# Cached keys, cached values and broadcast queries loaded through GpSimd's queue

## The chip, the core and the metric

The kernel runs on one core of a Trainium2 chip. The metric is device time in microseconds from start to end of the program. The kernel before takes 1567.99 us, the median of 3 runs (1566.31 to 1571.45).

A core has five engines that each take instructions from a queue of their own, in order: TensorE (PE, with weight loads shown as PEld), VectorE (DVE), ScalarE (ACT), GpSimd (POOL) and SyncE (SP). A DMA is issued by an instruction that stands in the queue of one of these engines; the bytes are then moved by 16 DMA engines that all issuers share. In the kernel before, nearly all transfers are issued from SP, some stores from ACT, and none from POOL.

## The reference

One step of a two-layer decoder trunk for a prompt of 512 tokens and for 8 sample sequences of 8 tokens with 2048 tokens of history. Layer 0 mixes tokens by dilated attention, layer 1 by a diagonal state-space layer; each is followed by a gated feed-forward block. The change lies in the attention of the sample sequences, which reads cached keys and values:

```python
DIL_GROUPS = ((128, 1), (512, 4), (2048, 16))     # (window, dilation)
def dilated_block(q_blk, kv_all, qi, dilation, n_keys):
    idx = qi[:, None] - dilation * jnp.arange(n_keys)[None, :]
    kvg = jnp.take(kv_all, jnp.maximum(idx, 0), axis=1)
    ...
    s = jnp.einsum('bqhd,bqkhd->bqhk', q_blk, kf) * (HEAD_DIM ** -0.5)
    lse = jax.nn.logsumexp(s, axis=-1)
    o = jnp.einsum('bqhk,bqkhd->bqhd', jnp.exp(s - lse[..., None]), vf)
# per token: softmax over the three groups' lse, weighted sum of the three o, then @ w_o
```

For each of 8 sequences and each of the three groups the scores need the cached keys at the group's stride, and the outputs need the cached values at the same places. New caches, shifted by 8 tokens, are outputs too.

## The kernel before

**Stages.** The program runs through these stages, one after the other on TensorE:

- 0 to about 300 us: the projection to queries, keys and values. Nine chunks of 512 columns; each weight piece (`raw`, L87) is split into a high and a low part (ACT L99, DVE L100) and multiplied in three passes (L353 to L355). Between the pieces the scores of the sample sequences are computed: group 2 on VectorE (`products`, L394: a tile of cached keys `kc` times a tile of queries `qb` copied to all 128 partitions, L399, then a sum per head, L401), groups 1 and 0 on TensorE (`score`, transposes L486, products L490 and L493).
- about 300 to 329 us: the rest of the scores of group 0 (eight sequences, one tile of 256 KB each).
- 329 to about 461 us, called the attention stage here: `attn_phase`. Four pairs of heads of the prompt (`prompt_pair`: scores L631, L634, L638, softmax on ACT and DVE, transposes L647, outputs L654 and L660) and eight decodes (`decode`, one for each sequence: seven tiles of cached values, 3328 KB in all, multiplied in L700, closed by L703 and a transpose L707). The last three sequences' scores of group 2 are computed here as well, now with the multiplication on GpSimd (L399) and the sum on VectorE.
- 461 us to the end: output projection, feed-forward, state-space layer, feed-forward. These stages load no cached keys or values.

**Buffers.** Cached keys, cached values and broadcast queries share a pool `kst` of six buffers of 512 KB, all named `kc`; the group-2 products of the attention stage have four buffers of their own in pool `kpa`, also named `kc`. Weights have four `raw` buffers.

**What sets the order.** The code says what depends on what; a scheduler, which plays the program through with its own estimate of each instruction's duration, then writes one fixed order per engine. Every engine works its order off without overtaking: an instruction that waits for a semaphore holds up all that stand behind it on the same engine. SP's order mixes the weight pieces (L87), the cached tiles (L390), the broadcast queries (L398), the prompt's values `vt` (three loads of 1 MB each, L588), a mask `mp` (512 KB, L586), the samples' new values `vn` (L690) and copies of the caches to the outputs (L83).

Of the kernel before, what the change touches and what calls it, by code (L numbers as in the profile page):

```python
# [29 lines left out]
WIN = (128, 512, 2048)  # L30
# [10 lines left out]
def dram(ap, off, dims):  # L41
    return bass.AP(tensor=ap.tensor, offset=ap.offset + off, ap=[list(d) for d in dims])
# [339 lines left out]
CACHES = ("cache_kv_w128", "cache_kv_w512", "cache_kv_w2048")  # L382
# [4 lines left out]
def cache_tile(nc, A, pool_, name, gi, b, c0, n, kv):  # L387
    t = pool_.tile([128, 2, 512], F32, name=name)[:, :n]
    st = STRIDE[gi]
    nc.sync.dma_start(t, dram(A[CACHES[gi]], (b * WIN[gi] + c0) * 1024 + kv * 512, [[st * 1024, 128], [1024, n], [1, 512]]))  # L390
    return t


def products(nc, A, L, eng, kst, P, b, part):  # L394
    c0 = 2 * part
    kc = cache_tile(nc, A, kst, "kc", 2, b, c0, 2, 0)
    qb = kst.tile([128, 2, 512], F32, name="kc")
    nc.sync.dma_start(qb, dram(L["qscr"], (b * 8 + c0) * 512, [[0, 128], [512, 2], [1, 512]]))  # L398
    eng.tensor_tensor(kc, kc, qb, OP.mult)  # L399
    for c in range(2):  # L400
        nc.vector.tensor_reduce(P[:, :, 0:2, c0 + c], kc[:, c].rearrange("p (a h d) -> p a h d", a=4, h=2), AX.X, OP.add)  # L401
# [17 lines left out]
def qkv_phase(nc, tc, A, es, L):  # L419
# [36 lines left out]
    def score2(b, part):  # L456
        if part == 0:
            prods[b] = dk.tile([128, 4, 4, 8], F32, name="P2", bufs=1)
            g.memset(prods[b], 0.0)
        products(nc, A, L, v, kst, prods[b], b, part)  # L460
        if part == 3:
            close2(nc, L, dk, psd, "Sd", prods.pop(b), b)

    def score(gi, b):
# [14 lines left out]
        for c0 in range(0, n, 2):  # L479
            w = min(2, n - c0)  # L480
            kc = cache_tile(nc, A, kst, "kc", gi, b, c0, w, 0)
            for c in range(w):
                u = c0 + c
                kp = ptp.tile([128, 4, 128], F32, name="pt")
                for hp in range(4):
                    te.transpose(kp[:, hp, :], kc[:, c, hp * 128:(hp + 1) * 128], ident)  # L486
                ks = dk.tile([128, 4, 128], F32, name="ks")
                s.activation(ks, kp, AF.Copy)
                for hp in range(4):
                    te.matmul(Sd[hp * 32:hp * 32 + 32, 0:128], Q[:, u, hp, :], ks[:, hp, :], start=u == 0, stop=u == n - 1,  # L490
                              tile_position=(0, hp * 32), skip_group_check=True)
# [100 lines left out]
def attn_phase(nc, tc, A, es, L):  # L592
# [71 lines left out]
    def decode(b):  # L664
# [28 lines left out]
        for gi in (0, 1, 2):  # L693
            for c0 in range(0, UNITS[gi], 2):
                w = min(2, UNITS[gi] - c0)
                vc = cache_tile(nc, A, kst, "kc", gi, b, c0, w, 1)
                for c in range(w):
                    for hp in range(4):
                        pz = pa[:, hp, :] if u == 0 else Z[:, u - 1, hp, :]
                        te.matmul(O[hp * 32:hp * 32 + 32, :], pz, vc[:, c, hp * 128:hp * 128 + 128], start=u == 0, stop=False, tile_position=(0, hp * 32), skip_group_check=True)  # L700
                    u += 1
# [14 lines left out]
    def score2():  # L716
        if not rest:
            return
        b, part = rest.pop(0)
        if part == 0:  # L720
            prods[b] = dk.tile([128, 4, 4, 8], F32, name="P2", bufs=1)
            g.memset(prods[b], 0.0)
        products(nc, A, L, g, kp, prods[b], b, part)
        if part == 3:
            close2(nc, L, dk, pD, "Sd", prods.pop(b), b)
# [628 lines left out]
```

## Time and profile before

| | |
|---|---|
| median of 3 runs | 1567.99 us |
| profiled execution, time / span | 1569.92 us / 1568.1 us |
| TensorE busy | 1517.8 us (97%) |
| VectorE busy | 917.3 us (58%) |
| ScalarE busy | 522.0 us (33%) |
| GpSimd busy | 320.6 us (20%) |
| DMA packets of SP's queue | 57.0% of the 16 engines' span, 305.86 MB |
| cached tiles issued (L390) | 96 of 512 KB, 16 of 256 KB |
| broadcast queries issued (L398) | 32 of 512 KB |

The span runs from the first to the last instruction. Busy time of TensorE includes modelled ends, so a busy TensorE is not one at its peak. DMA issues are not counted as busy time of the engine that issues them; a row such as `SPq` shows them.

### The profile page before, as it was taken

The page shows a single profiled execution, that of the slowest core. Times are in us where ns is not written, and L with a number is a line of the kernel's source. Part 1 is how long each engine was busy: PE and PEld are TensorE (multiplying, and loading weights), DVE is VectorE, ACT ScalarE, POOL GpSimd, SP SyncE. Part 2 cuts the span into 40 slices and gives each one's busy share as a digit, 9 for nine tenths or more (in the row PEclk, how much of TensorE's full clock was granted, in tenths as well). Part 3 has the DMA queues.
Part 4 walks back from the last instruction along what each step waited for, and adds up shares of the span by engine and source line. Part 5 has one row for each costly group of instructions (what it writes and reads, how often), then busy time and mean ns, then how long its engine had stood idle before and what let it go on. Part 6 is the DMA issues. An engine that isn't in the chain of part 4 may idle for free.

```text
span 1568.1 us, 28963 instructions
## 1 busy us (share of the span) xinstructions
PE 1517.8 (97%) x12038; PEld 1405.5 (90%) x12038; DVE 917.3 (58%) x1661; ACT 522.0 (33%) x774; POOL 320.6 (20%) x343
## 2 busy tenths in 40 slices
PE   9989899889979999999999999999999999999998
PEld 7878688656659999999999999999999999999998
DVE  5788954558727865388869666764343333333332
ACT  4524344634415221222212254343242212221222
POOL 2000102323203013845335420021011001000100
PEclk9999999988979999999999999899999999999999
DMA  7396853797985656488676665865545556442212
GB/s 264 129 368 229 268 186 108 230 349 248 322 265 162 221 195 222 165 314 285 243 242 235 240 223 183 269 181 202 218 164 208 192 187 217 154 144 81 81 62 81
DMA packets 194323, 326.79 MB, mean 208 GB/s; under 512 B 39568, under 2 KB 137104, under 8 KB 192656
## 3 DMA queue, kind: packets, MB, share of 16 engines
q1 hardware_dynamic: 184112, 305.86, 57.0%
q10 hardware_dynamic: 10080, 19.08, 3.5%
q8 instruction: 94, 1.54, 0.4%
q14 instruction: 37, 0.30, 0.1%
HBM read 291.31 MB, written 120.88 MB: 263 GB/s over the span
## 4 chain that ended last, share of the span: by engine, by line
PE 53%; DVE 2%; DMA 1%; ACT 0%; issue 0%; ACTq 0%; DVEq 0%
PE acc L106 49%; PE aux L106 1%; DMA u_scr<-uP 1%; DVE cb L1048 1%; DVE kk L1057 1%; PE acc L1138 1%; PE acc L1176 0%; PE acc L1177 0%; PE aux L1041 0%; PE aux L1177 0%; PE aux L1052 0%; PE aux L1176 0%; PE aux L814 0%; DVE Z L1158 0%; PE aux L1058 0%
## 5 line engine op out<-in xcount | busy, mean ns | idle before, releaser
L100 DVE TENSOR_TENSOR wlo<-raw,whi 128x1024 fp32r<-128x1024 f32 x200 | 247.1, 1236 | 274.3 <-ACT whi L99 266.6
L99 ACT ACTIVATE whi<-raw 128x1024 fp32r<-128x1024 f32 x200 | 208.1, 1042 | 515.6 <-PE acc L106 401.6
L106 PE MATMUL acc<-xgl,whi 128*128 128x288 f32 x1760 | 378.9, 296 | 0.0
L106 PE MATMUL acc<-xgh,whi 128*128 128x288 f32 x1760 | 377.2, 296 | 0.1
L106 PE MATMUL acc<-xgh,wlo 128*128 128x288 f32 x1760 | 377.2, 295 | 0.0
L106 PEld LDWEIGHTS acc<-xgl,whi 128*128 128x128 f32 x1760 | 282.7, 188 | 1.2 <-issue 1.0
L106 PEld LDWEIGHTS acc<-xgh,wlo 128*128 128x128 f32 x1760 | 282.9, 188 | 0.6 <-issue 0.2
L106 PEld LDWEIGHTS acc<-xgh,whi 128*128 128x128 f32 x1760 | 281.5, 188 | 0.5 <-DVE gt L791 0.3
L793 POOL TENSOR_TENSOR gt<-gt,rstd 128x576 f32<-128x576 f32 x44 | 79.9, 1817 | 429.0 <-ACT gt L792 428.9
L106 PE MATMUL acc<-hh,whi 128*128 128x288 f32 x704 | 151.3, 296 | 0.0
L106 PE MATMUL acc<-hh,wlo 128*128 128x288 f32 x704 | 151.2, 295 | 0.0
L106 PE MATMUL acc<-hl,whi 128*128 128x288 f32 x704 | 150.8, 295 | 0.0
L354 PE MATMUL acc<-wlo,xh 128*128 128x512 f32 x288 | 115.5, 403 | 3.4 <-DVE wlo L100 3.4
L353 PE MATMUL acc<-whi,xh 128*128 128x512 f32 x288 | 108.4, 400 | 5.6 <-ACT a L569 4.2
L106 PEld LDWEIGHTS acc<-hh,wlo 128*128 128x128 f32 x704 | 113.1, 188 | 0.2 <-issue 0.2
L106 PEld LDWEIGHTS acc<-hl,whi 128*128 128x128 f32 x704 | 113.0, 188 | 0.2 <-issue 0.2
L106 PEld LDWEIGHTS acc<-hh,whi 128*128 128x128 f32 x704 | 113.1, 188 | 0.0
L355 PE MATMUL acc<-whi,xl 128*128 128x512 f32 x288 | 112.9, 399 | 0.0
L191 POOL TENSOR_TENSOR ssum<-ssum,sq 128x576 f32<-128x576 f32 x21 | 36.1, 1717 | 180.8 <-ACT sq L190 180.8
L353 PEld LDWEIGHTS acc<-whi,xh 128*128 128x128 f32 x288 | 54.6, 191 | 19.1 <-ACT a L569 5.1
L354 PEld LDWEIGHTS acc<-wlo,xh 128*128 128x128 f32 x288 | 55.3, 192 | 15.7 <-DVE wlo L100 4.4
L355 PEld LDWEIGHTS acc<-whi,xl 128*128 128x128 f32 x288 | 55.3, 192 | 11.2
(351 smaller groups left out, 2017.4 us busy)
## 6 DMA issues: line engine op xcount, KB each, us to landing
o_kv_s<-cache_kv_w SPq DMA_DIRECT2D x64, 1020.0 KB
kc<-cache_kv_w SPq DMA_DIRECT2D x96, 512.0 KB
raw<-ffn_w_gate SPq DMA_DIRECT2D x44, 512.0 KB
raw<-ffn_w_up SPq DMA_DIRECT2D x44, 512.0 KB
raw<-ffn_w_down SPq DMA_DIRECT2D x40, 512.0 KB
raw<-w_qkv SPq DMA_DIRECT2D x36, 512.0 KB
kc<-qscr SPq DMA_DIRECT2D x32, 512.0 KB
o_kv_s<-cache_kv_w SPq DMA_DIRECT2D x16, 1008.0 KB
```

Source lines behind the costliest of these rows:

```text
L99: s.activation(hi, raw, AF.Copy)
L100: mark[0] = v.tensor_tensor(lo, raw, hi.bitcast(F32), OP.subtract)
L106: te.matmul(ps[:, c, :HN], w, x[:, c * HN:(c + 1) * HN], start=first and i == 0, stop=last and i == 2)
L191: g.tensor_tensor(self.ss, self.ss, sq, OP.add)
L353: te.matmul(ps[t], ah, wh[:, k2, :], start=k == 0, stop=False)
L354: te.matmul(ps[t], ah, wl[:, k2, :], start=False, stop=False)
L355: te.matmul(ps[t], al, wh[:, k2, :], start=False, stop=k == KT - 1)
L793: g.tensor_tensor(t, t, nin.r, OP.mult)
L1048: v.tensor_copy(cb[i][hs, :, gl, :], c[hs, qs, :])
L1057: v.scalar_tensor_tensor(k7, dmask, dcol[:, f:f + 1], k7, op0=OP.mult, op1=OP.add)
L1138: te.matmul(S[gl * 64:gl * 64 + 64, ri, q * 72:q * 72 + 72], Wc[:, ri, q, gl * 64:gl * 64 + 64], U[:, 2 * q + gl, :], start=True, stop=True)
```

## The change

The two lines that issue the loads of cached tiles and of broadcast queries name GpSimd instead of SyncE. All 112 loads of L390 and all 32 of L398 move: 144 DMAs. Weights, `vt`, `mp`, `vn` and the copies to the outputs stay on SP.

```diff
 def cache_tile(nc, A, pool_, name, gi, b, c0, n, kv):
     t = pool_.tile([128, 2, 512], F32, name=name)[:, :n]
     st = STRIDE[gi]
-    nc.sync.dma_start(t, dram(A[CACHES[gi]], ...))
+    nc.gpsimd.dma_start(t, dram(A[CACHES[gi]], ...))
     return t
...
     qb = kst.tile([128, 2, 512], F32, name="kc")
-    nc.sync.dma_start(qb, dram(L["qscr"], ...))
+    nc.gpsimd.dma_start(qb, dram(L["qscr"], ...))
     eng.tensor_tensor(kc, kc, qb, OP.mult)
```

Since the scheduler runs again, the order of the engines changes with it, up to the end of the attention stage; behind it all orders are as before. Three places matter.

SP at the entry to the attention stage, before. `kc` are cached tiles, `vt` the prompt's values, `mp` a mask, `o_kv_s` an output copy:

```order
L83 DMA o_kv_s<-cache_kv_w 16x16320
L390 DMA kc<-cache_kv_w 128x512 x2
L586 DMA mp<-c_mp 128x2048
L588 DMA vt_3181<-vtscr 128x4x512
L390 DMA kc<-cache_kv_w 128x512
L588 DMA vt_3180<-vtscr 128x4x512
L588 DMA vt_3179<-vtscr 128x4x512
L390 DMA kc<-cache_kv_w 128x512 x4
L390 DMA kc<-cache_kv_w 128x2x512 x6
```

With the change the copy, the mask and the three `vt` loads follow each other on SP, and the `kc` loads stand on POOL.

POOL in the attention stage, before (multiplications of the group-2 products, and small set-up of the next sequence):

```order
L399 TENSOR_TENSOR kc<-kc 128x1024 x5
L722 MEMSET P_3820 128x128
L407 MEMSET Q_4012 128x128
L410 COPY Q_4012<-qT_86 64x4x8 x2
L399 TENSOR_TENSOR kc<-kc 128x1024 x4
```

The same place on POOL with the change, from its fifth multiplication of the stage on:

```order
L399 TENSOR_TENSOR kc<-kc 128x1024
L722 MEMSET P_3820 128x128
L407 MEMSET Q_4012 128x128
L390 DMA kc<-cache_kv_w 128x2x512
L410 COPY Q_4012<-qT_86 64x4x8 x2
L399 TENSOR_TENSOR kc<-kc 128x1024
L390 DMA kc<-cache_kv_w 128x2x512
L398 DMA kc<-qscr 128x1024
L390 DMA kc<-cache_kv_w 128x512
L390 DMA kc<-cache_kv_w 128x2x512 x5
L398 DMA kc<-qscr 128x1024
L399 TENSOR_TENSOR kc<-kc 128x1024
```

The multiplications now stand between the loads of cached values, and a load behind a multiplication is issued only when that has run.

PE at the end of the attention stage, before. `O<-P_0`, `O<-P_1` are the last outputs of the prompt's last pair, `Sd<-kc` the products of a decode:

```order
L700 MATMUL Sd<-kc,pa 32x128 x4
L647 MATMUL pt<-ident,sm 128x128 x4
L700 MATMUL Sd<-kc,Pz_3218 32x128 x40
L654 MATMUL O<-P_4990,vt_3180 64x128
...
L707 MATMUL Sd<-ident,os 128x128
L673 MATMUL Sd<-ident,Sall 128x128 x3
L676 MATMUL Sd<-ident,pw 24x128
L700 MATMUL Sd<-kc,pa 32x128 x4
L700 MATMUL Sd<-kc,Pz_3217 32x128 x48
```

With the change, behind the last of the prompt's outputs:

```order
L660 MATMUL O<-P_1_4797,vt_3179 64x4x32
L412 MATMUL Sd<-ident,P_4309 128x128
L414 MATMUL Sd<-kT_89,Q_4501 32x8 x4
L673 MATMUL Sd<-ident,Sall 128x128 x3
L676 MATMUL Sd<-ident,pw 24x128
L700 MATMUL Sd<-kc,pa 32x128 x4
L700 MATMUL Sd<-kc,Pz_3218 32x128 x48
L703 MATMUL Sd<-vn,pn 32x128 x4
L707 MATMUL Sd<-ident,os 128x128
```

Before, two decodes stood behind the prompt's last pair and the one ahead of them ran inside it; now all three stand behind it. At the stage's entry PE's order has moved too: 44 products of the first decode (L700) stand ahead of the prompt's first scores (L634), where 20 stood before.

More of the change, by code (lines that the diff above doesn't have):

```diff
@@ L389, in cache_tile @@
     st = STRIDE[gi]
-    nc.sync.dma_start(t, dram(A[CACHES[gi]], (b * WIN[gi] + c0) * 1024 + kv * 512, [[st * 1024, 128], [1024, n], [1, 512]]))
+    nc.gpsimd.dma_start(t, dram(A[CACHES[gi]], (b * WIN[gi] + c0) * 1024 + kv * 512, [[st * 1024, 128], [1024, n], [1, 512]]))
     return t
@@ L397, in products @@
     qb = kst.tile([128, 2, 512], F32, name="kc")
-    nc.sync.dma_start(qb, dram(L["qscr"], (b * 8 + c0) * 512, [[0, 128], [512, 2], [1, 512]]))
+    nc.gpsimd.dma_start(qb, dram(L["qscr"], (b * 8 + c0) * 512, [[0, 128], [512, 2], [1, 512]]))
     eng.tensor_tensor(kc, kc, qb, OP.mult)
```

## The prediction

> **What bounds the kernel now.** First the busy times by stage (columns: time, then busy us and number of instructions of PE, PEld, DVE, ACT, POOL, then granted clock, DMA share, GB/s):
>
> ```profile
> 0.00:300.00 300.00, 284.83 (x1578) 228.61 (x1578) 216.52 (x377) 131.62 (x194) 36.39 (x96) 0.98 0.65 221
> 300.00:329.00 29.00, 20.33 (x332) 14.86 (x332) 4.59 (x31) 12.72 (x23) 4.95 (x25) 0.82 0.92 324
> 329.00:395.00 66.00, 63.10 (x767) 41.11 (x754) 53.41 (x175) 28.54 (x76) 22.32 (x13) 0.92 0.81 284
> 395.00:437.00 42.00, 41.97 (x655) 28.77 (x654) 30.24 (x121) 18.12 (x52) 7.93 (x7) 1.00 0.85 296
> 437.00:461.00 24.00, 16.01 (x255) 9.37 (x251) 2.55 (x19) 2.58 (x8) 0.00 (x0) 0.72 0.82 274
> 461.00:1568.00 1107.00, 1091.54 (x8473) 1082.83 (x8473) 610.04 (x939) 328.40 (x422) 248.99 (x203) 0.99 0.56 193
> ```
>
> Behind 461 us TensorE works without a break, nothing there is moved, and the orders are the same: I take this part as unchanged. The 300 us of the projection are TensorE's as well (95% busy). What is open lies from 300 to 461 us: there the DMA engines are 81 to 92% busy, and at 437 to 461 us TensorE is idle a third of the time.
>
> Next, what SP's one queue costs today. The list of waits up to 329 us has three rows that could be laid to it:
>
> ```profile
> ACT whi L99 <- DMA raw<-w_qkv: 4.4, 1, 4.4
> PE acc L354 <- DVE wlo L100: 3.4, 2, 3.0
> PE pt L486 <- DMA kc<-cache_kv_w: 7.4, 2, 3.7
> ```
>
> A weight piece came late once in 300 us, and TensorE waited for a split weight twice, for 3.4 us in all. So weights that stand behind cached tiles on SP are hardly a cost. The 7.4 us are two waits for a cached tile at the entry to the attention stage, and SP's timeline and PE's show why:
>
> ```profile
> 307.64 0.33 SPq L586 DMA_DIRECT2D mp<-c_mp  x1
> 308.02 0.43 SPq L588 DMA_DIRECT2D vt<-vtscr  x1
> 308.55 0.45 SPq L390 DMA_DIRECT2D kc<-cache_kv_w  x1
> 309.05 1.18 SPq L588 DMA_DIRECT2D vt<-vtscr  x2
> ...
> 315.35 0.41 PE L486 MATMUL pt<-ident,kc 128*128 128x128 f32 x2 [3.74 <-DMA kc<-cache_kv_w]
> ...
> 322.63 0.69 PE L486 MATMUL pt<-ident,kc 128*128 128x128 f32 x2 [3.62 <-DMA kc<-cache_kv_w]
> ```
>
> The small cached tiles of the last scores stand in one line with 3584 KB (3.67 MB) of `mp` and `vt`. At the 324 GB/s of the second row above these take 11.3 us. This is the gain that a queue of their own could bring.
>
> **What POOL takes on.** In the attention stage SP issues these loads, first for 329 to 395 us, then for 395 to 461 us:
>
> ```profile
> L390 SPq DMA_DIRECT2D kc<-cache_kv_w x29: 346/394/1177, 328.3 to 393.9; - x29
> L398 SPq DMA_DIRECT2D kc<-qscr x10: 325/349/948, 329.5 to 391.5; - x10
> ...
> L390 SPq DMA_DIRECT2D kc<-cache_kv_w x31: 350/380/1912, 396.1 to 452.9; - x31
> L398 SPq DMA_DIRECT2D kc<-qscr x2: 349/425/501, 401.6 to 407.7; - x2
> ```
>
> That is 39 and 33 DMAs. No row shows what one costs POOL, so I bound it by rows:
>
> ```profile
> 124.38 0.64 ACTq L375 DMA_DIRECT2D o_kv_s<-o  x1
> ...
> 18.36 0.53 POOL L447 TENSOR_TENSOR C<-cs,gq 128x160 f32<-128x160 f32 x1 [16.14 <-DMA gq<-q_norm]
> ...
> L399 POOL TENSOR_TENSOR kc<-kc 128x1024 f32<-128x1024 f32 x12 | 28.7, 2395 | 58.5 <-DMA kc<-qscr 45.6 <-DMA kc<-cache_kv_w 10.8 <-DVE P L401 2.1
> ```
>
> Below: 0.39 us, as on SP; ACT pays 0.64 us. Above: 2.4 us, a whole pass of POOL over 1024 elements. Between them I take SP's 0.34 us, plus one step per row of the load at POOL's pace in L447 (0.53 us / 160 = 3.3 ns): 256 rows of 2 KB for a cached tile of 512 KB, 128 rows of 4 KB for the queries, so 1.19 and 0.76 us. [...]
>
> By stage: 29 x 1.19 + 10 x 0.76 = 42.1 us, and with the 22.3 us that POOL works already 64.4 of 66 us; then 31 x 1.19 + 2 x 0.76 + 7.9 = 46.3 of 66 us. So POOL is just full in the first half and has room in the second. In the first half it also waits: a multiplication stands one or two loads behind its own queries, and loads stand behind it. One such pair today:
>
> ```profile
> 342.16 0.35 SPq L398 DMA_DIRECT2D kc<-qscr  x1
> ...
> 349.80 2.35 POOL L399 TENSOR_TENSOR kc<-kc 128x1024 f32<-128x1024 f32 x1 [7.63 <-DMA kc<-qscr]
> ```
>
> 7.6 us from issue to use, under full DMA engines. I take 5 us and two loads in between, so some 2.6 us of standing still, for three or four of the first multiplications: 9.6 us. POOL then needs 74 us in a stretch of 66: **+8 us**. Bounds: 0 (price as on SP: 15 + 22 = 37 us) and, at 2.4 us, 39 x 2.4 + 22.3 - 66 = 50 us and 33 x 2.4 + 7.9 - 66 = 21 us more, +71.
>
> [...]
>
> **The order's own cost.** PE's new order puts a third decode behind the prompt's last pair. What a decode costs there is read from the ends of the last three:
>
> ```profile
> 438.00 0.33 PE L707 MATMUL Sd<-ident,os 128*128 128x128 f32 x1
> 450.42 0.47 PE L707 MATMUL Sd<-ident,os 128*128 128x128 f32 x1 [0.46 <-ACT os L705]
> 460.27 0.33 PE L707 MATMUL Sd<-ident,os 128*128 128x128 f32 x1 [0.46 <-ACT os L705]
> ```
>
> 12.4 and 9.9 us, 11.1 on average, against 3328 KB (3.41 MB) / 274 GB/s = 12.4 us: they run at the pace of the loads. The cover that hid the third was the prompt's work. Taking its matmuls out of the pair gives something back, at most 8 us of PE work (16.0 / 2) at clock 0.72, or 5.8 at full clock, since PE was full there (41.97 of 42); I take half. **+11.1 - 2.9 = +8.2 us** (5.3 to 11.1).
>
> At the entry 24 more products, three tiles of eight (each program instruction has two records), stand ahead of the prompt's first scores:
>
> ```profile
> 328.59 0.41 PE L634 MATMUL S<-kT,att 64*32 64x256 f32 x2
> ...
> 333.49 0.65 PE L700 MATMUL Sd<-kc,Pz 128*32 128x128 f32 x16
> ```
>
> The scores begin 334.1 - 328.6 = 5.5 us later if the loads keep their pace, 0 if the prompt catches up: **+2.8 us**.
>
> **The gain.** `kc` on a queue of its own no longer stands behind `vt`: between -7.4 us and 0, since the same 3.67 MB still pass through the same DMA engines and each score now needs POOL for its load too: **-3.7 us**.
>
> [...]
>
> **The projection.** Of the 144 loads some 58 are issued here (20 of them queries), beside 36.4 us of POOL's work: 38 x 1.19 + 20 x 0.76 = 60 us more, so POOL is a third full. Products there run on VectorE, which waited 5.3 us for queries; TensorE is not behind these directly. Bounds -3.4 (the split weights come in time) and +5.3; I take **0**.
>
> **Sum:** 8 + 8.2 + 2.8 - 3.7 = +15.3 us on the profiled execution's 1569.92 us (span 1568.1 and 1.8 us around it), 1585.2. That execution is 1.9 us above the median, so 1583 against 1567.99.
>
> **The rivals.**
>
> - *POOL becomes the bound.* From about 1.1 us per load (66 - 22.3 over 39) it is full, and each further 0.1 us costs 4 us. At 1.8 us: 39 x 1.8 + 22.3 - 66 = 26.5, 33 x 1.8 + 7.9 - 66 = 1.3, with the 9.6 us of waits and 7.3 us for order and gain (8.2 + 2.8 - 3.7) 45 us: 1613. At 2.4 us: 71 + 7.3 = 78 us, about 1646. [...] Against it: ACT's 0.64 us. Chance 0.16.
> - *VectorE holds POOL up.* [...] Chance 0.06. [...]
> - *Faster.* The tiles' own queue keeps the DMA engines fuller in the tail. At the 324 GB/s seen at the entry a decode takes 10.5 us, and with six of the 21 tiles drawn ahead while the prompt's pair ends, three take 15 / 21 x 31.5 = 22.5 us, as long as two now (22.3). Then what is left is -7.4 and -3.4 us: 1557. For it: PE's waits in the attention stage are for tiles (below). Against it: POOL's multiplications stand between. It decides if a load costs POOL under about 0.6 us. Chance 0.15.
>
> ```profile
> PE Sd L700 <- DMA kc<-cache_kv_w: 5.7, 10, 1.3
> ```
>
> - *No change.* The issue is cheap (0.6 us: 23 + 22 = 45 us of 66, nothing added), the third decode costs its lower end and the gain is whole: 5.3 + 2.8 - 7.4 = +0.7, so 1569. Chance 0.17.
>
> **How the numbers follow.** Likeliest, with 0.46: 1583 us, its own range 1573 to 1600. Slower by over 0.3% (4.7 us, about what this kernel's runs can tell from none): 0.46 + 0.16 + 0.06 = 0.68. Within: 0.17. Faster: 0.15. The range 1558 to 1628 leaves out half of the faster case and half of POOL as the bound.
>
> **What would show it.** Right: rows of L390 on POOL's queue between 0.7 and 1.3 us; POOL close to full from 329 to 395 us; three decode ends 10 to 12 us apart behind the last L660; the stage from 461 us on as long as before. Wrong: POOL half idle in that stretch; decodes under 9 us each; the waits at L486 gone and nothing in their place; or a stall of several us in the projection, where VectorE's sums wait for a `P` that POOL clears behind a load.

## The result: 1586.9 us against 1567.2 us

The changed kernel takes 1586.86 us (median of 4 runs, 1583.12 to 1589.97) against 1567.15 us before (4 runs). The ratio is 1.0123, with a 95% interval of 1.0088 to 1.0157: slower by 14 to 25 us. The profiled execution of the changed kernel took 1583.12 us, its span is 1581.3 us.

The busy times by stage of the changed kernel, with the columns of the prediction's first table (time; busy us and instructions of PE, PEld, DVE, ACT, POOL; granted clock; DMA share; GB/s):

```profile
0.00:300.00 300.00, 283.14 (x1582) 227.31 (x1582) 219.67 (x377) 131.94 (x195) 76.82 (x155) 0.99 0.68 225
300.00:329.00 29.00, 21.18 (x328) 15.95 (x332) 4.28 (x29) 11.92 (x22) 14.42 (x39) 0.81 0.89 310
329.00:395.00 66.00, 64.74 (x704) 42.27 (x697) 48.35 (x164) 25.26 (x69) 38.85 (x44) 0.82 0.71 240
395.00:437.00 42.00, 40.39 (x531) 26.16 (x531) 30.70 (x112) 18.48 (x50) 27.62 (x31) 0.97 0.90 308
437.00:475.00 38.00, 30.11 (x412) 19.99 (x411) 7.62 (x39) 5.66 (x17) 11.28 (x16) 0.63 0.64 214
475.00:1581.00 1106.00, 1089.08 (x8498) 1079.51 (x8498) 610.80 (x940) 328.43 (x423) 246.11 (x203) 1.00 0.58 193
```

The 44 instructions that POOL has from 329 to 395 us, 13 before, include the loads. With them POOL is busy for 38.9 of 66 us: not full. TensorE is busy for 64.7 of 66 us, a little more than before, and yet does fewer instructions in that time (704 against 767), at a granted clock of 0.82 where it had 0.92.

What one load costs POOL (duration of the issuing instruction, min/median/max in ns):

```profile
L390 POOL DMA_DIRECT2D kc<-cache_kv_w x112: 537/716/880, 17.2 to 470.4; - x112
L398 POOL DMA_DIRECT2D kc<-qscr x32: 547/574/697, 70.0 to 424.7; - x32
```

At the entry to the attention stage the two waits of 3.74 and 3.62 us at L486 are gone, since the mask and the prompt's values now follow each other on SP. In their place PE's timeline has three others, 5.2 us together:

```profile
314.69 0.83 PE L673 MATMUL Sd<-ident,Sall 128*128 128x128 f32 x3 [1.90 <-DVE Sall L615]
317.25 0.66 PE L490 MATMUL Sd<-ks,Qz 128*32 128x128 f32 x8 [0.87 <-POOL Qz L477]
...
325.63 0.64 PE L700 MATMUL Sd<-kc,Pz 128*32 128x128 f32 x16 [2.44 <-DMA kc<-cache_kv_w]
```

At the end of the stage three decodes stand behind the prompt's last pair, as its order said:

```profile
444.77 2.77 PE L660 MATMUL O<-P,vt 128*64 128x128 f32 x22
...
456.93 0.47 PE L707 MATMUL Sd<-ident,os 128*128 128x128 f32 x1 [0.46 <-ACT os L705]
467.69 0.48 PE L707 MATMUL Sd<-ident,os 128*128 128x128 f32 x1 [0.46 <-ACT os L705]
476.75 0.33 PE L707 MATMUL Sd<-ident,os 128*128 128x128 f32 x1 [0.46 <-ACT os L705]
478.68 0.61 PE L106 MATMUL acc<-ath,whi 128*128 128x288 f32 x1 [1.60 <-ACT ath L742]
```

By such ends and starts the 13.2 us between the two profiled spans divide as follows.

| stretch | before | after | difference |
|---|---|---|---|
| start to the last product of the projection (L353) | 289.4 | 286.2 | -3.2 |
| from there to the prompt's first scores (L634) | 39.2 | 44.5 | +5.3 |
| the prompt's four pairs, to the last L660 | 109.2 | 116.4 | +7.2 |
| from there to the output projection (L106) | 24.1 | 31.6 | +7.5 |
| the rest | 1106.2 | 1102.6 | -3.6 |

POOL's list of waits from 329 to 478 us shows its queue standing in order:

```profile
POOL kc L390 <- PE Sd L700: 34.3, 14, 10.8
POOL kc L399 <- DMA kc<-qscr: 6.7, 5, 4.8
POOL kc L398 <- DVE P L401: 6.3, 2, 3.9
```

34.3 us are loads of values that wait for a free buffer. Before, a load that waited on SP held up only DMAs, since SP's rows from 285 to 470 us are DMA issues alone; here it also holds up the multiplications behind it: two loads at 390.56 us waited 7.33 us for TensorE's L700, and the next multiplication, behind them, starts at 394.85 us. That was the first theory of the loss.

### The profile page after: what moved, and what is told of

Same layout as the page of the kernel before. It is cut to its first block, busy times and chain, and to the rows that moved or that the text cites. A ratio compares the mean times of both kernels' runs of the same rounds, so it can differ in the third digit from the quotient of the medians.

```text
span 1581.3 us, 28983 instructions
## 1 busy us (share of the span) xinstructions
PE 1528.6 (97%) x12038; PEld 1411.2 (89%) x12038; DVE 921.4 (58%) x1661; ACT 521.7 (33%) x774; POOL 415.1 (26%) x487
## 3 DMA queue, kind: packets, MB, share of 16 engines
q0 software_dynamic: 19712, 71.31, 13.2%
## 4 chain that ended last, share of the span: by engine, by line
PE 50%; DVE 2%; DMA 1%; ACT 0%; issue 0%; ACTq 0%; DVEq 0%
PE acc L106 47%; PE aux L106 1%; DMA U<-u_scr 1%; DVE cb L1048 1%; DMA y_scr<-ys 0%; DVE kk L1057 0%; PE aux L1041 0%; PE acc L1138 0%; PE aux L1052 0%; PE aux L814 0%; PE acc L1177 0%; PE acc L1176 0%; DVE Z L1158 0%; PE aux L1058 0%; PE aux L196 0%
## 5 line engine op out<-in xcount | busy, mean ns | idle before, releaser
L106 PE MATMUL acc<-xgl,whi 128*128 128x288 f32 x1760 | 378.6, 296 | 1.0 <-DVE xgl L171 1.0
L106 PE MATMUL acc<-xgh,wlo 128*128 128x288 f32 x1760 | 377.8, 296 | 0.0
L106 PE MATMUL acc<-xgh,whi 128*128 128x288 f32 x1760 | 377.1, 296 | 0.1
L106 PEld LDWEIGHTS acc<-xgl,whi 128*128 128x128 f32 x1760 | 282.7, 188 | 2.5 <-DVE xgl L171 1.3
L106 PEld LDWEIGHTS acc<-xgh,wlo 128*128 128x128 f32 x1760 | 282.8, 188 | 0.6 <-issue 0.2
L106 PEld LDWEIGHTS acc<-xgh,whi 128*128 128x128 f32 x1760 | 281.8, 188 | 0.5 <-DVE gt L791 0.3
L106 PE MATMUL acc<-hh,whi 128*128 128x288 f32 x704 | 151.3, 296 | 0.0
L106 PE MATMUL acc<-hh,wlo 128*128 128x288 f32 x704 | 151.3, 295 | 0.0
L106 PE MATMUL acc<-hl,whi 128*128 128x288 f32 x704 | 151.0, 295 | 0.0
L390 POOL DMA_DIRECT2D kc<-cache_kv_w x112 | 78.1, 698 | 165.1 <-PE pt L486 61.9
L106 PEld LDWEIGHTS acc<-hh,wlo 128*128 128x128 f32 x704 | 113.1, 188 | 0.2 <-issue 0.2
L106 PEld LDWEIGHTS acc<-hl,whi 128*128 128x128 f32 x704 | 113.0, 188 | 0.2 <-issue 0.2
L106 PEld LDWEIGHTS acc<-hh,whi 128*128 128x128 f32 x704 | 113.0, 188 | 0.0
L353 PE MATMUL acc<-whi,xh 128*128 128x512 f32 x288 | 107.7, 399 | 2.4 <-ACT xh L276 2.3
L354 PEld LDWEIGHTS acc<-wlo,xh 128*128 128x128 f32 x288 | 54.6, 189 | 16.3 <-DVE wlo L100 5.2
L353 PEld LDWEIGHTS acc<-whi,xh 128*128 128x128 f32 x288 | 54.7, 191 | 15.0 <-ACT xh L276 2.9
```

What stands on the lines that cost most here:

```text
L106: te.matmul(ps[:, c, :HN], w, x[:, c * HN:(c + 1) * HN], start=first and i == 0, stop=last and i == 2)
L353: te.matmul(ps[t], ah, wh[:, k2, :], start=k == 0, stop=False)
L354: te.matmul(ps[t], ah, wl[:, k2, :], start=False, stop=False)
L390: nc.gpsimd.dma_start(t, dram(A[CACHES[gi]], (b * WIN[gi] + c0) * 1024 + kv * 512, [[st * 1024, 128], [1024, n], [1, 512]]))
```

## The experiments

All times are medians. Each ratio is to the runs of the kernel before that were made beside it, and the us by which a kernel exceeds the kernel before are worked out from it; they can lie up to 3 us from the difference of the two medians.

**The first theories.** A: the loss is the order that the scheduler writes (three decodes in the tail instead of two) plus POOL's queue standing in order in the attention stage. B: each load moved lands later because GpSimd issues it, so each part of the change costs in proportion to its loads.

### The new tail alone

All loads stay on SP; the last three decodes are written behind the prompt's last pair. The rest of TensorE's order is as before.

```diff
...
+                    last[0] = te.matmul(O[h * 64:h * 64 + 64, :, b, :], ...
...
-    for hp in range(4):
-        decode(2 * hp)
-        prompt_pair(hp, score2)
-        decode(2 * hp + 1)
+    for x in (0, "p0", 1, 2, "p1", 3, 4, "p2", "p3"):
+        prompt_pair(int(x[1]), score2) if isinstance(x, str) else decode(x)
+    with tc.issue_after(last[0].ins):
+        for b in (5, 6, 7):
+            decode(b)
```

> The kernel before, all loads on SP, but with the last three decodes put behind the prompt's last pair, as the change's order has them; everything ahead of the tail stands as before. Theory A (half of the loss is the order that the scheduler writes): the tail from the last L660 to the last L707 grows from 22.5 us to about 30 us, the time by 5 to 9 us, about 1574. Theory B (the loss is the path of the loads: issued and spelled out by GpSimd, they land later): no change, 1567 within 3 us.

Measured: 1575.08 us, ratio 1.0039 (1.0005 to 1.0073), 6 us. The step of the tail has the size that A gave it.

### The new tail taken away

The changed kernel, with decode 5 put ahead of the last outputs of the prompt's last pair, so that two decodes are left behind it.

```diff
+            with tc.issue_after(done[5].ins) if (hp, r) == (3, 2) else ExitStack():
                 for gi in (1, 2):
...
+            done[b] = te.matmul(O[hp * 32:hp * 32 + 32, :], pn[:, hp * 32:hp * 32 + 32], ...
```

> The changed kernel with one order taken back: the sixth decode (b = 5) stands ahead of the last two blocks of the prompt's last pair on TensorE, so that two decodes and not three are left at the end; queues and loads as with the change. Theory A: the tail is back at 20 to 24 us and 5 to 8 us of the 19 are won back, about 1579. Theory B: nothing is won, 1587 within 3 us, since the loads of that decode are late wherever its matmuls stand.

Measured: 1585.84 us, ratio 1.0109 (1.0066 to 1.0152). The tail shrinks, to 20.4 us from the last L660 to L106, but the prompt's pairs with the decode in them now take 124.7 us, and nearly all of the loss stays. A's terms do not simply add.

### Only the loads ahead of the attention stage on POOL

```diff
+    q = nc.gpsimd if eng is nc.vector else nc.sync
-    kc = cache_tile(nc, A, kst, "kc", 2, b, c0, 2, 0)
+    kc = cache_tile(nc, A, kst, "kc", 2, b, c0, 2, 0, q)
...
-            kc = cache_tile(nc, A, kst, "kc", gi, b, c0, w, 0)
+            kc = cache_tile(nc, A, kst, "kc", gi, b, c0, w, 0, nc.gpsimd)
```

> Only the loads ahead of the attention stage (cached keys and queries of the projection stage and of the group-0 scores, 64 of the 144 DMAs) are issued from GpSimd; the attention stage's products and all cached values stay on SP. Theory A (the harm is in the attention stage, where multiplications and value loads share GpSimd's queue): no loss, and the 3 to 4 us that the changed kernel was ahead at the end of the scores (321.8 against 325.9 us) stay, so 1563 to 1567. Theory B (each load moved costs its later landing): 64 / 144 of the 19 us, about 1575.

Measured: 1572.38 us, ratio 1.0032 (1.0009 to 1.0056). A small loss where A expected none or a gain; the 8 us of B lie just inside the interval.

### Only keys and queries, and only values, on POOL

```diff
-    nc.sync.dma_start(t, dram(A[CACHES[gi]], ...
+    (nc.sync if kv else nc.gpsimd).dma_start(t, dram(A[CACHES[gi]], ...
-    nc.sync.dma_start(qb, ...
+    nc.gpsimd.dma_start(qb, ...
```

> Cached keys and broadcast queries from GpSimd (88 DMAs), cached values on SP. On GpSimd the multiplications of the attention stage then stand behind their own loads alone, and the order leaves two decodes at the end as before. Theory A: 1564 to 1570, as before or a little better. Theory B: 88 / 144 of the 19 us, about 1579.

Measured: 1570.22 us, ratio 1.0026 (0.9992 to 1.006): 88 of the 144 loads moved, and no difference that can be told. B falls: it asked for 12 us, and the interval ends at 9. The other 56 alone, with `(nc.gpsimd if kv else nc.sync)` and the queries on SP:

> Only the 56 loads of cached values go to GpSimd's queue; keys and broadcast queries stay on SyncE's. The order that results also has three decodes behind the prompt's last pair (two before). Theory A (the loss is the order plus value loads standing in order among the multiplications): 6 us for the third decode, as the run that had only that order showed, and 4 to 6 us of value loads held behind multiplications and behind full buffers, so 1577 to 1581 us, most of the whole change's loss, although it is 56 loads of 144. Theory B (each load moved costs alike): 56/144 of 19 us, so about 1574 us, and nothing in the queue's waits that stands out. Where the time is lost: by A between the prompt's first scores and the last decode's end.

Measured: 1577.36 us, ratio 1.0049 (1.0018 to 1.0081), 8 us. Both theories gave about this.

### The multiplications off POOL

If value loads lose time behind POOL's multiplications, these can be taken away. The same edit on the kernel before is the control.

```diff
-        products(nc, A, L, g, kp, prods[b], b, part)
+        products(nc, A, L, v, kp, prods[b], b, part)
```

> Control with all loads on SyncE's queue: the attention stage's multiplications and sums of keys and queries run on VectorE and not on GpSimd. Both theories: VectorE, busy 28 of 66 us in that stage before, takes some 35 us more over 130 us of stage, so 0 to 10 us over the kernel before: 1566 to 1577 us.

> The changed kernel with the attention stage's multiplications and sums on VectorE, so that GpSimd's queue there has the loads and little beside them; the order that results has one decode behind the prompt's last pair (three in the changed kernel). Theory A: with neither the multiplications among the loads nor the long tail, the loss against its control (the same edit with SyncE's loads) shrinks from 19 to 0 to 8 us; about 1570 to 1580 us. Theory B: the same 144 loads land just as late, 15 to 20 us over its control, 1583 to 1592 us.

Measured: control 1571.82 us, ratio 1.0029 (1.0008 to 1.005); changed kernel 1591.99 us, ratio 1.015 (1.0115 to 1.0185). The difference is 20 us, as large as without the edit, with no multiplications on POOL and one decode in the tail. **Theory A's forecast fails** too, and the list of waits does not carry its reading: on POOL the wait of loads for buffers is now longer (59.4 us in the row below, 34.3 in the changed kernel's), although no multiplication stands behind these loads any more. What this run does not rule out is a loss by order, since this kernel too has an order of its own: the prompt's four pairs take 146 us in its trace, 117 in the changed kernel's and 125 in the control's.

```profile
POOL kc L390 <- PE Sd L700: 59.4, 22, 12.2
```

### More issues on POOL

```diff
+    if kv and n == 2:
+        for c in range(2):
+            nc.gpsimd.dma_start(t[:, c], dram(A[CACHES[gi]], (b * WIN[gi] + c0 + c) * 1024 + kv * 512, ...))
+        return t
```

> The changed kernel with each value load of two units issued as two transfers of half the size: 48 issues more on GpSimd's queue, some 30 of them in the attention stage, 0.55 us each by the rows of its trace, 16 us of GpSimd there. Theory A (GpSimd has room, 38.9 us busy of 66, and what is lost is standing in order): at most 5 us over the changed kernel, 1585 to 1592 us. Rival C (GpSimd's issuing itself is the bound): 10 to 16 us more, 1597 to 1603 us.

Measured: 1600.78 us, ratio 1.0204 (1.0174 to 1.0234), 14 us over the changed kernel, in the range of C. But the trace says something else. POOL is busy for 38.9 of the following 54.6 us, and TensorE sits at half clock for all of them, though it is shown busy for 50.9:

```profile
325.60:380.20 54.60, 50.93 (x354) 28.70 (x352) 35.55 (x103) 13.55 (x37) 38.88 (x47) 0.50 0.69 230
```

The edit had also moved the order: all 52 products of the first decode (104 records) now stand ahead of the prompt's first scores. So this run does not separate C from the order.

### What the traces have in common

So the granted clock was read more closely. In the traces of the kernel before and of the changed kernel it is either 1.00 or 0.50, and up to the attention's end it is 0.50 for 3.4 us or a multiple of that (3.4, 6.8, 10.2, 13.7 and 17.1 us). Before, one such period lies in the prompt's first pair, behind a pause of TensorE (1.45 of 3.4 us busy):

```profile
350.60:354.00 3.40, 1.45 (x14) 0.85 (x15) 3.40 (x7) 0.73 (x2) 3.23 (x2) 1.00 0.23 70
354.00:364.20 10.20, 10.20 (x65) 7.62 (x65) 8.13 (x25) 2.91 (x8) 0.67 (x1) 0.50 0.30 93
364.20:367.60 3.40, 3.40 (x35) 2.03 (x32) 2.07 (x8) 1.82 (x5) 2.63 (x3) 0.99 0.77 284
```

TensorE's records slow down with it. The same four transpositions take 1.12 us inside this period and 0.66 us right behind it:

```profile
355.71 1.12 PE L647 MATMUL pt<-ident,sm 128*128 128x128 f32 x4
...
364.45 0.66 PE L647 MATMUL pt<-ident,sm 128*128 128x128 f32 x4
```

In the changed kernel the first pair has two. The first of them follows 3.4 us in which TensorE is shown fully busy, with little but the prompt's scores:

```profile
335.30:338.70 3.40, 3.40 (x36) 1.87 (x29) 2.71 (x11) 1.22 (x4) 0.77 (x2) 1.00 0.88 253
338.70:348.90 10.20, 10.20 (x51) 6.46 (x50) 6.94 (x17) 2.67 (x7) 6.69 (x5) 0.50 0.77 284
348.90:352.30 3.40, 3.40 (x32) 1.95 (x30) 3.13 (x13) 2.17 (x6) 0.49 (x1) 0.99 0.68 230
```

Over all four pairs, first of the kernel before and then of the changed one:

```profile
328.00:438.00 110.00, 107.07 (x1465) 71.22 (x1456) 83.95 (x298) 46.94 (x129) 30.26 (x20) 0.95 0.83 289
```

```profile
331.00:447.00 116.00, 112.89 (x1262) 74.14 (x1247) 82.22 (x283) 45.84 (x124) 67.22 (x75) 0.85 0.73 248
```

A mean clock of 0.95 over 110 us is 11 us at half clock; 0.85 over 116 us is 35 us. TensorE is busy for 97% of both, so this is where a half clock can cost directly, at most 12 us for the 24 us more; against it stands that one decode's work has left the stretch.

This gave two questions. Is it the order or the queue? And is the half clock a cause or a sign?

### Order and queue, each alone

The names of the instructions are the same in both kernels, so each can be held to the other's order on TensorE, VectorE and ScalarE, from the projection to the attention's end, with edges that fix the order of issue and add no wait. POOL and SP are left to the scheduler, which writes them an order that neither kernel has.

```diff
     with tile.TileContext(nc, schedule_with_timeline_sim=True) as tc:
         build(nc, tc, aps)
+        put_in_order(nc, tc)
...
+        for p, q in zip(rows, rows[1:]):
+            tc.add_manual_dep(mine[q], mine[p].name, how, reason="order")
```

> The kernel before (all loads on SyncE's queue), with TensorE, VectorE and ScalarE held to the order that the changed kernel has, from the projection to the attention's end. Theory O: the loss comes with the order, 1580 to 1592 us, and about 68 us at half clock after 290 us. Theory Q: 1564 to 1573 us. Half of each: about 1577 us.

> The changed kernel (144 loads on GpSimd's queue), with TensorE, VectorE and ScalarE held to the order in which the kernel before has their work, from the projection to the attention's end. Theory O (what costs is the order that comes with the change, because TensorE then sits at half clock longer: 68 us after 290 us in the changed kernel's trace, 37 us before): the time of the kernel before, 1564 to 1573 us, and about 37 us at half clock. Theory Q (the queue itself costs, whatever the order): the changed kernel's 1580 to 1592 us. Half of each: about 1577 us.

Measured:

| | order of before | order of after |
|---|---|---|
| loads on SP | 1 | 1.0113 (1.0092 to 1.0135), 1583.49 us |
| loads on POOL | 1.0059 (1.0034 to 1.0085), 1575.81 us | 1.0123 (1.0088 to 1.0157), 1586.86 us |

**The new order, with no load moved, loses 18 us**, as much as the whole change within the uncertainty. The queue with the old order loses 9 us. The two do not add up to more (27 us) when both are there. Theory O is not all: by it the kernel with the old order should have come out at 1564 to 1573 us. Of the half-clock times that it named, the 68 us came (68 us from 290 us to the output projection, loads on SP, new order), and the 37 us did not (55 us, loads on POOL, old order, in a run whose clock of 0.978 is below that kernel's median of 0.983).

The 18 us can't be put down to the order that the change has, though. In the trace of the kernel with the loads on SP and the new order, VectorE waits 7.2 us for a tile that POOL clears (L722) behind its multiplications, one of which waited for its queries; the softmax of the prompt stands behind that in VectorE's order, and TensorE pauses for 5.0 us:

```profile
372.45 2.34 POOL L399 TENSOR_TENSOR kc<-kc 128x1024 f32<-128x1024 f32 x1 [3.48 <-DMA kc<-qscr]
374.73 0.20 POOL L722 MEMSET P<- 128x128 f32 x1
...
374.97 1.28 DVE L401 TENSOR_REDUCE P<-kc 128x8 f32<-128x512 f32 x2 [7.16 <-POOL P L722]
...
377.85 1.09 PE L647 MATMUL pt<-ident,sm 128*128 128x128 f32 x4 [5.03 <-DVE rd L614]
```

Then the clock stays at half for 27.3 us, which can cost up to 13.7 us, more than the pause:

```profile
374.20:377.60 3.40, 0.00 (x0) 0.00 (x0) 2.63 (x8) 0.81 (x2) 1.28 (x5) 1.00 0.48 131
377.60:404.90 27.30, 27.05 (x185) 16.05 (x189) 16.32 (x57) 8.54 (x24) 4.71 (x2) 0.50 0.60 210
```

On POOL, seven multiplications of the stage stand ahead of this clearing here. In the kernel before and in the changed kernel there are five, and in the changed kernel's trace nothing waits for the clearing. So this stall belongs to the experiment and not to the change, and how much of the 18 us the change pays for its order stays open. What was timed without such a stall is the third decode, 6 us.

### The half clock, cause or sign

Products that do nothing for the result are put ahead of the transpositions of the first pair, into a bank that these overwrite. They add work and no transfer.

```diff
                 pt = pP.tile([128, 4, 128], F32, name="pt")
+                for _ in range(5 if hp < 1 else 0):
+                    FILL.append(te.matmul(pt[:, 0:2].rearrange("p a b -> p (a b)"), L["ones"].bitcast(BF16)[:, 0:128], L["ones"].bitcast(BF16), start=True, stop=True).ins)
                 for c in range(4):
```

> The changed kernel, its TensorE, VectorE and ScalarE held to their own order, with five bf16 products of 128x256 more ahead of each transposition of the prompt's first pair's probabilities (40 in all, over the whole array; what they write is overwritten, nothing of the result changes). [...] Theory H (half clock in the prompt's pairs is what the order costs): the first pair, 20 us at half clock in the changed kernel's trace, has 0 to 7, which gives back 7 to 10 us and pays 2 to 6: 1578 to 1586 us. Rival W (it is the waits themselves, the clock is only a sign of them): the time goes up by the products, 1589 to 1595 us, whatever the clock does.

Measured: 1578.58 us, ratio 1.007 (1.0042 to 1.0097), where the changed kernel has 1.0123. The first pair, changed kernel and then with the products:

```profile
331.00:371.00 40.00, 38.74 (x313) 24.45 (x298) 28.44 (x90) 14.70 (x40) 22.88 (x24) 0.73 0.64 213
```

```profile
330.00:371.00 41.00, 37.65 (x375) 24.66 (x372) 32.15 (x99) 15.52 (x42) 23.17 (x24) 0.95 0.66 217
```

The clock goes from 0.73 to 0.95, and in 41 us TensorE now gets through 375 instructions, 40 of them the added ones, instead of 313 in 40 us. The time falls by about 8 us although work was added, where W had it rise. No row shows what one added product costs; the 2 to 6 us that H has for them, here and in the next run, are the author's estimate. The intervals of the two ratios overlap a little, so the size is uncertain. The clock rose in every run: 0.978 to 0.985 in the eleven with the products, 0.972 to 0.975 in the four without. In the two traces the prompt's pairs take 113 us with the products and 117 without, with 11 instead of 35 us at half clock.

This speaks for the half clock as a cause of part of the loss. It does not settle it, because the products are not the only difference. TensorE, VectorE and ScalarE have the changed kernel's order, but POOL's was written anew: between 362 and 399 us two multiplications stand ahead of loads that they followed there, and two loads of values stand further ahead.

> The same 40 products put into the version in which only the loads ahead of the attention stage are on GpSimd's queue, held to its own order; its trace had 31 us at half clock in the first pair (334 to 365 us) and the shortest tail of all. Theory H: the half clock there falls to 0 to 10 us, which gives back 10 to 15 us and pays 2 to 6: 1560 to 1568 us, so possibly below the kernel before. Rival W: 1574 to 1580 us.

Measured: 1570.01 us, ratio 1.0023 (0.9997 to 1.0049), against 1.0032 without the products: no gain that can be told. The clock of the first pair did come back, from 0.62 to 0.96 in the traces below (without and with the products). H expected 10 to 15 us from that and missed; W, with 1574 to 1580 us, missed as well. This is the cleaner of the two pairs, since here all five engines have the same order with and without the products, by the names and shapes in the two traces.

```profile
327.00:367.00 40.00, 40.00 (x279) 23.57 (x265) 26.90 (x79) 12.28 (x33) 11.34 (x5) 0.62 0.62 222
```

```profile
332.00:372.00 40.00, 38.74 (x404) 25.19 (x396) 29.02 (x94) 16.06 (x43) 14.98 (x10) 0.96 0.76 263
```

One reason shows when the clock of every run is listed, not of the profiled one alone: the runs without the products had a median clock of 0.9835, the profiled one 0.979. Its 31 us at half clock were probably more than that kernel usually has, so there was little to win back. In the two profiled executions the prompt's pairs are 4.8 us shorter with the products (119.6 against 124.4 us), and the stretch from the projection to the first scores is 4.9 us longer.

### All kernels by their clock

"Clock loss" is (1 - mean granted clock) x span, the median over a kernel's runs: an upper bound for what the clock took, since a slower TensorE costs only where it is the bound.

| kernel | ratio to before | runs | clock | clock loss, us |
|---|---|---|---|---|
| before | 1 | 75 | 0.983 | 26.6 |
| the change | 1.0123 | 4 | 0.973 | 42.8 |
| new tail alone | 1.0039 | 10 | 0.9805 | 30.7 |
| change, tail taken away | 1.0109 | 4 | 0.9715 | 45.1 |
| loads ahead of the attention | 1.0032 | 10 | 0.9835 | 25.9 |
| keys and queries | 1.0026 | 10 | 0.9845 | 24.4 |
| values | 1.0049 | 6 | 0.9805 | 30.7 |
| before, multiplications on VectorE | 1.0029 | 10 | 0.981 | 29.9 |
| change, multiplications on VectorE | 1.015 | 4 | 0.9715 | 45.3 |
| change, value loads halved | 1.0204 | 4 | 0.966 | 54.4 |
| SP, order of after | 1.0113 | 6 | 0.976 | 38.0 |
| POOL, order of before | 1.0059 | 9 | 0.983 | 26.8 |
| change with products | 1.007 | 11 | 0.983 | 26.8 |
| loads ahead of the attention, products | 1.0023 | 12 | 0.986 | 22.0 |

The change has 16 us more clock loss than the kernel before and takes 19 us more. All kernels at 1.01 and above have a clock of 0.976 or less, and none of the others has. An estimate: at 0.64 us of time for each us of clock loss, as among the runs of the kernel before (last section), 16 us are worth about 10 us, and 9 are left, as many as the queue loses with the old order. That the two go together does not show which causes which.

Three things stay open. One run of the kernel with halved value loads has a clock of 0.922, over 120 us of clock loss, and its time, 1598.65 us, lies among those of that kernel's other three; so a run's mean clock alone does not give its time. How much the order costs that the change has is open, as said. And the 9 us of the queue with the old order are not in the clock (0.983, as before), nor are the 11 us of the change with products (0.983). In the first of these, TensorE's waits for values are little longer than the 5.7 us before:

```profile
PE Sd L700 <- DMA kc<-cache_kv_w: 7.6, 11, 1.9
```

VectorE's waits for POOL's multiplications from 329 to 440 us have grown more, from 0.3 us in the kernel before (first row) to 5.8 us, and TensorE waits 1.9 us for the softmax (L614), where it had no such wait. That is not 9 us, so where the rest lies is not settled.

```profile
DVE P L401 <- POOL kc L399: 0.3, 1, 0.3
...
DVE P L401 <- POOL kc L399: 5.8, 2, 4.8
```

And no version beat the kernel before: the best two are level with it.

## Why the prediction was right in its time and wrong in a term

The forecast was 1583 us with a range of 1573 to 1600; 1586.9 lies in it. Its mechanism is half right, and the sum owes its closeness in part to luck: one term stood for something that did not happen, and other terms erred in both directions.

- **POOL filling in the first half, +8: this step failed.** It had 1.19 and 0.76 us for a load, the author's estimate from one step of 3.3 ns per row; no run shows such a step. Measured are 0.72 and 0.57 us. By the step's own sum POOL needs 29 x 0.72 + 10 x 0.57 + 22.3 + 9.6 = 58.5 of 66 us, so the term would have been 0; the trace has 38.9 us busy, 59%. "POOL half idle in that stretch" was named as what would show it wrong, and that is nearly so. The prompt's pairs are longer all the same, by 7.2 us, with 35 instead of 11 us at half clock. That the term had the right size is chance: the prediction read TensorE's clock in its first table (0.92, 1.00, 0.72), used it to price one decode's matmuls, and had no term for a change of it.
- **The third decode, +8.2: right.** The three end 9.8, 10.8 and 9.1 us after one another, 29.7 us from the last L660 (447.1 us), where two took 22.5: +7.2. With this order alone on SP the time rose by 6 us. The price of one decode, 11.1 us, was somewhat high, and only one of the three lies in the 10 to 12 us that were named as the sign. The 2.9 us that the pairs were to win back do not show: they got longer, and putting the decode back into them brought nothing that can be told.
- **24 products ahead of the first scores, +2.8, and the gain at the entry, -3.7.** The waits at L486 went, as expected, and 5.2 us of others came. The stretch to the first scores is 5.3 us longer, where the two terms had it 0.9 shorter. So the gain from a queue of its own does not show in the time.
- **The projection, 0:** it ends 3.2 us earlier, inside the bounds given (-3.4 to +5.3). **Behind the stage** nothing was to change: -3.6 us.
- **The rivals.** "POOL becomes the bound" falls by its price, 0.72 us. "Faster" asked for under about 0.6 us a load and for fuller DMA engines; the price came near, but the DMA share from 329 to 395 us fell from 0.81 to 0.71. "No change" had its cheap issue and was still wrong: it took the gain at the entry as whole, the third decode at its lower end, and the prompt's pairs as unchanged. Whether VectorE holds POOL up was tested by no run, and the changed kernel's trace has no sign of it at a load's issue: the 17 loads of cached tiles whose issue runs beside a scaling of L615 cost POOL 0.72 us in the median, the other 95 cost 0.71, and the longest of all is 0.88 us.

## What to carry to other kernels

When a scheduler writes the order, moving a DMA to another queue is two changes: hold the order fixed and time each alone before blaming the queue. Hold it on every engine; here POOL's was left free, and the kernel meant to show the order alone stalled in a place where the changed kernel does not. Where TensorE is the bound in a stage of small products, read its granted clock there as a term of the sum of its own: behind pauses of 2 and 5 us (the kernel before; loads on SP with the new order) it stayed at half for 10 and 27 us here, which can cost up to 5 and 14 us. And take the clock from all runs, not from the profiled one.

## What the runs showed of the hardware that was not expected

- **The granted clock falls to one half and stays there in steps of 3.4 us**: 10.2 us in the rows above, 27.3, and once 54.6 us while TensorE is shown busy for 50.9 of them. It fell behind 374.2 to 377.6 us of the run with the loads on SP and the new order, in which no product ran. It also fell behind 3.4 us that were shown as fully busy (335.3 to 338.7 us, the changed kernel), and in the kernel with halved value loads 50 us of small products, shown as 93% busy, did not bring it back (ends of matmuls are modelled, so such a share can be too high). With forty bf16 products of 128x256 among the small ones the clock of the first pair was 0.95 and 0.96, without them 0.73 and 0.62.
- **The clock goes with a good part of the spread between runs.** Among 75 runs of the kernel before, the span rises by 0.64 us for each us of clock loss (correlation 0.88): 1561.2 us is the median of the 21 runs with a clock of 0.986 or more, 1572.3 us of the 13 with 0.978 or less.
- **What a load costs GpSimd follows its rows, not its bytes.** It is 0.72 us for 256 rows in 512 KB and 0.57 us for 128 rows in 512 KB (rows above), and 0.54 us for 128 rows in 256 KB, in the kernel with halved value loads:

```profile
L392 POOL DMA_DIRECT2D kc<-cache_kv_w x96: 539/539/774, 310.7 to 479.1; - x96
```

  That is about 1.2 ns a row, (0.72 - 0.57) / 128, beside some 0.4 us; the prediction had put 3.3 ns a row beside 0.34 us.
